# Low parts of the weights by a DMA that adds onto a tile written by ScalarE, instead of a subtraction on VectorE

## The chip, the cores and the metric

The kernel runs on one core of a Trainium2 chip. The core has TensorE (PE, matmuls, with PEld its weight loads), VectorE (DVE), ScalarE (ACT), GpSimd (POOL), SyncE (SP, here only issuing DMAs) and 16 DMA engines that all queues share. SBUF is the on-chip memory, PSUM holds matmul results, HBM is the chip's DRAM. The metric is the device time of one execution in microseconds; times are medians over runs. Each engine works through its own queue in order, and waits on semaphores of the others.

## The reference

Two transformer-like blocks run one after the other on 512 tokens of 1024 channels, all in float32. The first has two layers over the tokens and a context of 256 tokens (the context is updated only in layer 0), the second has one layer with a state-space (SSD) and a gated-delta branch.

```python
def trunk_layer(...):                      # first block, twice
    u  = (rmsnorm(x,  g_mix) * (1 + sc1)  + sh1)  @ w_in
    uc = (rmsnorm(cx, g_mix) * (1 + sc1c) + sh1c) @ w_in
    ...                                    # pooling, gated linear attention, attention
    x = x + ga1 * (mix @ w_out)
    x = x + ga2 * squared_relu_mlp(rmsnorm(x, g_mlp) * (1 + sc2) + sh2, w_up, w_down)
    if update_ctx:                         # the same for cx, 256 tokens
        ...
def squared_relu_mlp(h, w_up, w_down):
    return jnp.square(jax.nn.relu(h @ w_up)) @ w_down
def second_block(...):
    proj = h @ w_in[l]                     # 14400 columns
    ...                                    # SSD scan, gated delta rule, gates
    x = x + g1 * rmsnorm_2(merged @ w_out[l], norm_mix_post[l])
    y = jnp.square(jax.nn.relu(h @ w_mlp_up[l])) @ w_mlp_down[l]
    x = x + g2 * rmsnorm_2(y, norm_mlp_post[l])
```

Most of the arithmetic is products of activations with weight matrices of 1024 or 4096 rows.

## The kernel before

**Three products for one.** A float32 product is made of matmuls on the faster fp32r type. Each operand is split into a high part (rounded to fp32r) and a low part (the difference). `mm3` (lines 290 to 294) issues three matmuls: high times high (L292), a mixed product (L293), the other mixed product (L294).

**Weights.** A weight matrix is stored in DRAM as half tiles of 128 x 1024 floats (512 KB, 4 KB a partition), two of which make a group of 256 output columns. `whalf` (lines 273 to 283) brings one half: a DMA on SyncE's queue into `wraw` (three buffers), a rounding copy on ScalarE into `whi` (L281, two buffers), a subtraction raw minus high on VectorE into `wlo` (L282, two buffers). There are 503 halves in the run. Where the same weights serve two column parts, they are loaded once for each.

**Users.** `dense` takes weights as the stationary operand and activations of 512 or 256 columns as the moving one: per half 8 sets of three matmuls, and after the second half of a group two evacuations (for the up projections, ScalarE's relu, square and rounding copy, lines 1046, 1047 and 258). `tokens` takes the activations as stationary. The context MLP of layer 0, its output projection, and in the second block the output projection and the first groups of the up projection (`SPLITS`, `dense_parts`) run with 256 columns. Modulation vectors come from large weight rows too: by TensorE through `mraw` and `wraw` (L447, L444) or, in other stretches, by VectorE on rows that SyncE loads (L480, L484).

**Other traffic.** Block 2 writes many intermediates to DRAM and reads them back with another layout (on ScalarE's and SyncE's queues).

**GpSimd** does small work: it zeroes tiles (L723), takes the inverse roots of the norms (`root`, L392), and makes copies of one column that order buffers (L522).

**Order.** The code is written as a program; the Tile scheduler places the instructions on each engine's queue by a timeline it simulates. Weight splits are marked urgent (`urgent`), so they are placed early. The number of buffers of `wraw`, `whi` and `wlo` limits how far loads and splits run ahead of the matmuls.

## Time and profile before

| what | value |
|---|---|
| median of 3 runs | 3591.73 us (3591.07 to 3602.67) |
| profiled execution | 3592.06 us, its span 3590.1 us |
| granted TensorE clock, mean | 0.957 of 2.4 GHz |
| TensorE busy | 3392.4 us (94%) |
| VectorE busy | 2238.5 us (62%) |
| ScalarE busy | 1517.7 us (42%) |
| GpSimd busy | 58.5 us (2%) |
| DMA bytes | 492.55 MB, 137 GB/s over the span |

The profile is one execution. Busy times of an engine are sums over its instructions; matmuls overlap in the pipeline, so TensorE's busy time is not work at its peak. A wait is put down to the semaphore that came last. "Issue to landing" of a DMA is from its issue by the queue's engine to its completion.

### The profile page before, as it was taken

The numbers are of one execution on the slowest core, as the hardware profiler recorded it, in microseconds if no ns is written. First come the engines' busy times: TensorE is split into PE (matmuls) and PEld (weight loads), VectorE is DVE, ScalarE is ACT, GpSimd is POOL, SyncE is SP. The second block draws the span as 40 slices with busy tenths as digits, with TensorE's granted clock in tenths as the row PEclk, the third lists the DMA queues.
The fourth block names the chain that finished last, engine by engine and source line by source line (L and its number), as shares of the span: only waits on it lengthen the run. The fifth ranks groups of instructions, "written<-read, shape, count | busy, mean of one in ns | idle before, by whom it ended". The sixth has DMA issues, their size and how long they took to land.

```text
span 3590.1 us, 53732 instructions
## 1 busy us (share of the span) xinstructions
PE 3392.4 (94%) x20714; PEld 2823.2 (79%) x20714; DVE 2238.5 (62%) x4339; ACT 1517.7 (42%) x2675; POOL 58.5 (2%) x105
## 2 busy tenths in 40 slices
PE   7999999998999999989999999999899978999998
PEld 5787788887888797667888687788898757888886
DVE  3844787557533458866533779977866668663334
ACT  3523765453333355633333555453233323264333
POOL 0000000000000000000000000000000000000000
PEclk9799899999999998999999899999999979999999
DMA  6334123644622221036622356456456656453222
GB/s 226 119 125 151 54 80 104 222 135 147 194 100 96 99 71 34 7 117 195 201 95 91 120 180 179 147 165 196 144 180 193 213 185 188 154 185 130 94 94 76
DMA packets 268399, 492.55 MB, mean 137 GB/s; under 512 B 44912, under 2 KB 129904, under 8 KB 267888
## 3 DMA queue, kind: packets, MB, share of 16 engines
q1 hardware_dynamic: 214128, 447.17, 38.8%
q10 hardware_dynamic: 54016, 41.95, 3.5%
q8 instruction: 163, 2.67, 0.3%
q14 instruction: 92, 0.75, 0.1%
HBM read 431.22 MB, written 57.80 MB: 136 GB/s over the span
## 4 chain that ended last, share of the span: by engine, by line
PE 62%; issue 12%; DVE 11%; DMA 10%; ACT 3%; SPq 1%; POOL 0%; DVEq 0%; POOLq 0%; ACTq 0%
PE mm L292 15%; PE mm L293 15%; PE mm L294 15%; DMA mraw<-in_w_ada 2%; DVE wlo L282 2%; PE op L952 2%; PE sm L729 1%; DMA mraw<-in_w_late 1%; PE SC L447 1%; DVE AT L484 1%; DMA gG<-rowS 1%; PE SL L926 1%; ACT whi L281 1%; PE mm L590 1%; DVE svP L1498 1%
## 5 line engine op out<-in xcount | busy, mean ns | idle before, releaser
L282 DVE TENSOR_TENSOR wlo<-wraw,whi 128x1024 fp32r<-128x1024 f32 x503 | 614.2, 1221 | 519.2 <-ACT whi L281 514.9
L281 ACT ACTIVATE whi<-wraw 128x1024 fp32r<-128x1024 f32 x503 | 531.6, 1057 | 913.3 <-PE mm L293 727.4
L292 PE MATMUL mm<-h,whi 128*128 128x512 f32 (+1 forms) x2344 | 859.2, 369 | 23.7 <-ACT h L415 7.0
L293 PE MATMUL mm<-h,whi 128*128 128x512 f32 (+1 forms) x2344 | 852.2, 364 | 11.0 <-DVE h L416 9.8
L294 PE MATMUL mm<-h,wlo 128*128 128x512 f32 (+1 forms) x2344 | 835.7, 363 | 2.3 <-DVE wlo L282 2.0
L292 PEld LDWEIGHTS mm<-h,whi 128*128 128x128 f32 x2344 | 445.0, 190 | 108.7 <-ACT h L415 9.6
L293 PEld LDWEIGHTS mm<-h,whi 128*128 128x128 f32 x2344 | 446.1, 190 | 88.1 <-DVE h L416 17.9
L294 PEld LDWEIGHTS mm<-h,wlo 128*128 128x128 f32 x2344 | 444.0, 190 | 75.5 <-DVE wlo L282 4.8
L293 PE MATMUL mm<-wlo,h 128*128 128x256 f32 x1200 | 350.8, 293 | 16.7 <-DVE wlo L282 16.3
L292 PE MATMUL mm<-whi,h 128*128 128x256 f32 x1200 | 348.3, 293 | 10.9 <-ACT whi L281 7.8
L294 PE MATMUL mm<-whi,h 128*128 128x256 f32 x1200 | 343.9, 288 | 0.0
L293 PEld LDWEIGHTS mm<-wlo,h 128*128 128x128 f32 x1200 | 232.8, 194 | 28.7 <-DVE wlo L282 23.1
L292 PEld LDWEIGHTS mm<-whi,h 128*128 128x128 f32 x1200 | 231.6, 194 | 26.9 <-issue 11.0
L294 PEld LDWEIGHTS mm<-whi,h 128*128 128x128 f32 x1200 | 232.2, 194 | 14.1 <-issue 10.6
L292 PE MATMUL mm<-U,whi 128*128 128x512 f32 (+1 forms) x608 | 229.8, 379 | 1.3 <-DVE V L1076 1.3
L293 PE MATMUL mm<-U,whi 128*128 128x512 f32 (+1 forms) x608 | 227.0, 374 | 0.0
L294 PE MATMUL mm<-U,wlo 128*128 128x512 f32 (+1 forms) x608 | 222.9, 376 | 1.8 <-DVE wlo L282 1.8
L484 DVE SCALAR_TENSOR_TENSOR AT<-mraw,cst,AT 128x512 f32<-128x512 f32 x140 | 104.9, 750 | 96.7 <-DMA mraw<-in_w_ada 58.4
L292 PE MATMUL mm<-big,whi 128*128 128x512 f32 x384 | 154.2, 402 | 5.4 <-DVE fa L1826 2.4
L1286 DVE SCALAR_TENSOR_TENSOR fa<-fr,const,fa 128x511 f32<-128x511 f32 (+2 forms) x192 | 142.5, 750 | 26.0 <-ACT fa L1281 13.4
L293 PE MATMUL mm<-big,whi 128*128 128x512 f32 x384 | 153.4, 400 | 0.6 <-DVE big L259 0.6
L294 PE MATMUL mm<-big,wlo 128*128 128x512 f32 x384 | 150.0, 398 | 0.0
(570 smaller groups left out, 5059.4 us busy)
## 6 DMA issues: line engine op xcount, KB each, us to landing
wraw<-in_w_in SPq DMA_DIRECT2D x166, 512.0 KB, 3.5
wraw<-in_w_up SPq DMA_DIRECT2D x96, 512.0 KB, 3.3
wraw<-in_w_down SPq DMA_DIRECT2D x96, 512.0 KB, 3.4
mraw<-in_w_mod SPq DMA_DIRECT2D x96, 256.0 KB, 3.0
mraw<-in_w_ada SPq DMA_DIRECT2D x96, 256.0 KB, 2.9
wraw<-in_w_out SPq DMA_DIRECT2D x40, 512.0 KB, 3.3
wraw<-in_w_mlp_up SPq DMA_DIRECT2D x40, 512.0 KB, 3.3
mraw<-in_w_late SPq DMA_DIRECT2D x64, 256.0 KB, 2.8
```

What stands on the lines that cost most here:

```text
L281: nc.scalar.activation(hi, raw, AF.Copy)
L282: nc.vector.tensor_tensor(lo, raw, hi.bitcast(F32), op=ALU.subtract)
L292: nc.tensor.matmul(out, lh, rh, start=start, stop=False)
L293: nc.tensor.matmul(out, lh, rl, start=False, stop=False)
L294: nc.tensor.matmul(out, ll, rh, start=False, stop=stop)
L447: nc.tensor.matmul(ps[k % 4 * 32:k % 4 * 32 + 32, :256], st[:, k], raw[:, j * 256:(j + 1) * 256], start=(k < 4), stop=(k >= 4))
L484: nc.vector.scalar_tensor_tensor(acc, raw, st[:, k, 0:1], acc, op0=ALU.mult, op1=ALU.add)
L590: nc.tensor.matmul(ps[j * 32:j * 32 + 32], w[:, k * 32:k * 32 + 32], h[k][i % 2].bitcast(F32), start=(i == 0), stop=(i == 3))
L729: nc.tensor.matmul(gp[:, t], K[:, t], Q[:, t], start=True, stop=True)
L926: nc.tensor.matmul(at[i], qh[his], lo, start=False, stop=True)
L952: nc.tensor.matmul(op[j * 64:j * 64 + 64, pr * 128:(pr + 1) * 128], v[:, g * 64:(g + 1) * 64], pts[j][:, b * 128:(b + 1) * 128], start=(b ...
L1286: nc.vector.scalar_tensor_tensor(acc[:, d:], raw[:, :NL - d], w(j), acc[:, d:], op0=ALU.mult, op1=ALU.add)
```

## The change

The low part is no longer the difference of two tiles on VectorE. ScalarE reads the raw half a second time and writes its negated copy, rounded to fp32r in the same way, into `wlo`. Then a DMA on GpSimd's queue reads the same half from DRAM again and adds it onto `wlo`, which leaves raw minus high. `wraw` has two buffers instead of three, `wlo` three instead of two; the two other users of the `wraw` tag follow.

```diff
@@ whalf
-        raw = self.t([128, 1024], "wraw", 3)[:, :n]
+        raw = self.t([128, 1024], "wraw", 2)[:, :n]
         hi = self.t([128, 1024], "whi", 2, F32R)[:, :n]
-        lo = self.t([128, 1024], "wlo", 2, F32R)[:, :n]
+        lo = self.t([128, 1024], "wlo", 3, F32R)[:, :n]
         with self.urgent() if soon else nullcontext():
             nc.sync.dma_start(raw, self.A[name][i])
             nc.scalar.activation(hi, raw, AF.Copy)
-            nc.vector.tensor_tensor(lo, raw, hi.bitcast(F32), op=ALU.subtract)
+            nc.scalar.activation(lo, raw, AF.Copy, scale=-1.0)
+            nc.gpsimd.dma_start(lo, self.A[name][i], accum_op=ALU.add)
@@ modulation
-                raw = (self.spare.pop(0) if self.spare else self.t([128, 1024], "wraw", 3) if n == 4 else
+                raw = (self.spare.pop(0) if self.spare else self.t([128, 1024], "wraw", 2) if n == 4 else
@@ gla_proj
-        w = self.t([128, 1024], "wraw", 3)[:, :256]
+        w = self.t([128, 1024], "wraw", 2)[:, :256]
```

After line 282 the line numbers of the changed kernel are one higher: its L282 is ScalarE's second pass, L283 the adding DMA.

ScalarE's queue in the last groups of the context's up projection in layer 0 (256 columns), before; `ct` and `h` are the activations that are evacuated, the numbers count tiles:

```order
L281 ACTIVATE whi_6980<-wraw_6979 128x1024
L1046 ACTIVATE ct_6955<-mm_6905 128x256
L1047 ACTIVATE ct_6955<-ct_6955 128x256
L258 ACTIVATE h_932_5297<-ct_6955 128x256
L281 ACTIVATE whi_7010<-wraw_7009 128x1024
L1046 ACTIVATE ct_6972<-mm_6906 128x256
L1047 ACTIVATE ct_6972<-ct_6972 128x256
L258 ACTIVATE h_932_5297<-ct_6972 128x256
L281 ACTIVATE whi_7052<-wraw_7051 128x1024
```

The same place in the changed kernel:

```order
L282 ACTIVATE wlo_7086<-wraw_7084 128x1024
L1047 ACTIVATE ct_7029<-mm_6977 128x256
L1048 ACTIVATE ct_7029<-ct_7029 128x256
L281 ACTIVATE whi_7085<-wraw_7084 128x1024
L1047 ACTIVATE ct_7046<-mm_6978 128x256
L258 ACTIVATE h_932_5329<-ct_7029 128x256
L1048 ACTIVATE ct_7046<-ct_7046 128x256
L258 ACTIVATE h_932_5329<-ct_7046 128x256
L282 ACTIVATE wlo_7129<-wraw_7127 128x1024
L281 ACTIVATE whi_7128<-wraw_7127 128x1024
```

Of each half the negating pass now stands in front of the rounding pass, between evacuations of the groups before.

GpSimd's queue around the norm between the output projection and the MLP of the tokens in layer 0, before (`nr` is the inverse root of that norm):

```order
L674 MEMSET gst_8322 64x256 x2
L392 TENSOR_TENSOR nr_8061<-nv_8059,const_69 128x2
L873 COPY vc_8448<-U_294_1466 128x128 x2
L392 TENSOR_TENSOR nr_8787<-nv_8785,const_69 128x4
L423 MEMSET cst_14761 128x256
```

And the same norm in the changed kernel:

```order
L283 DMA wlo_8804<-in_w_out 128x1024
L283 DMA wlo_8835<-in_w_out 128x1024
L283 DMA wlo_8952<-in_w_up 128x1024
L283 DMA wlo_8983<-in_w_up 128x1024
L283 DMA wlo_9057<-in_w_up 128x1024
L393 TENSOR_TENSOR nr_8905<-nv_8903,const_69 128x4
L283 DMA wlo_9088<-in_w_up 128x1024
L283 DMA wlo_9162<-in_w_up 128x1024
```

The root now stands among the adding DMAs of the weights that are used before and after it.

## Rows read from the trace of the kernel before

**Rows 1.** The page's part 1: busy time, share of span, instructions.

```profile
span 3590.1 us, 53732 instructions
PE 3392.4 (94%) x20714; PEld 2823.2 (79%) x20714; DVE 2238.5 (62%) x4339; ACT 1517.7 (42%) x2675; POOL 58.5 (2%) x105
```

**Rows 2.** The page's part 4: chain that ended last, by engine, by line.

```profile
PE 62%; issue 12%; DVE 11%; DMA 10%; ACT 3%; SPq 1%; POOL 0%; DVEq 0%; POOLq 0%; ACTq 0%
PE mm L292 15%; PE mm L293 15%; PE mm L294 15%; DMA mraw<-in_w_ada 2%; DVE wlo L282 2%; PE op L952 2%; PE sm L729 1%; DMA mraw<-in_w_late 1%; PE SC L447 1%; DVE AT L484 1%; DMA gG<-rowS 1%; PE SL L926 1%; ACT whi L281 1%; PE mm L590 1%; DVE svP L1498 1%
```

**Rows 3.** Waits, whole span: who waited for whom, us, times, longest.

```profile
ACT whi L281 <- PE mm L293: 727.4, 285, 9.2
DVE wlo L282 <- ACT whi L281: 514.9, 248, 9.2
...
PE mm L293 <- DVE wlo L282: 16.3, 15, 2.3
...
PE mm L294 <- DVE wlo L282: 3.9, 3, 1.8
...
SPq L280 <- DVE wlo L282: 1471.7, 369, 26.8
```

**Rows 4.** Stretches: engines' busy us, clock, DMA share, GB/s; then L281 alone.

```profile
660.00:760.00 100.00, 98.79 (x816) 92.43 (x816) 56.27 (x80) 55.27 (x90) 0.00 (x0) 1.00 0.60 197
897.50:987.30 89.80, 87.87 (x402) 71.95 (x402) 53.79 (x76) 29.85 (x38) 0.32 (x1) 1.00 0.62 194
987.30:1077.00 89.70, 89.70 (x394) 73.59 (x393) 32.04 (x33) 32.29 (x42) 0.00 (x0) 1.00 0.29 99
...
660.00:760.00 100.00, 33.51 (x32) 1.00 0.60 197
897.50:987.30 89.80, 16.96 (x16) 1.00 0.62 194
987.30:1077.00 89.70, 16.98 (x16) 1.00 0.29 99
```

**Rows 5.** Groups of instructions by line and form: count, busy us, mean ns.

```profile
L282 DVE TENSOR_TENSOR wlo<-wraw,whi 128x1024 fp32r<-128x1024 f32 x503 | 614.2, 1221 | 519.2 <-ACT whi L281 514.9
L281 ACT ACTIVATE whi<-wraw 128x1024 fp32r<-128x1024 f32 x503 | 531.6, 1057 | 913.3 <-PE mm L293 727.4
...
L292 PE MATMUL mm<-h,whi 128*128 128x256 f32 x736 | 212.0, 292 | 2.5 <-ACT h L415 1.3 <-ACT whi L281 0.5 <-DVE h L1076 0.4
...
L292 PE MATMUL mm<-U,whi 128*128 128x256 f32 x96 | 26.8, 284 | 0.0
```

**Rows 6.** ScalarE in order of time, narrow up projection: start, duration, what.

```profile
684.16 0.39 ACT L1046 ACTIVATE ct<-mm 128x256 f32<-128x256 f32 x1 [0.47 <-PE mm L294]
684.58 0.42 ACT L1047 ACTIVATE ct<-ct 128x256 f32<-128x256 f32 x1
685.03 0.42 ACT L258 ACTIVATE U<-ct 128x256 fp32r<-128x256 f32 x1
```

**Rows 7.** DMA issues: count, KB each, median us from issue to landing.

```profile
wraw<-in_w_up SPq DMA_DIRECT2D x96, 512.0 KB, 3.3
...
wraw<-in_w_gdn_up SPq DMA_DIRECT2D x16, 512.0 KB, 4.8
```

**Rows 8.** One stretch of the start-up: engines' busy us, clock, DMA share, GB/s.

```profile
8.00:22.00 14.00, 12.58 (x84) 7.04 (x80) 3.28 (x10) 2.83 (x8) 0.71 (x1) 1.00 1.02 414
```

**Rows 9.** The page's part 2: DMA rate in 40 equal slices.

```profile
GB/s 226 119 125 151 54 80 104 222 135 147 194 100 96 99 71 34 7 117 195 201 95 91 120 180 179 147 165 196 144 180 193 213 185 188 154 185 130 94 94 76
```

**Rows 10.** GpSimd's longest wait by the waits view of that engine.

```profile
POOL nr L392 <- DVE nv L380: 1663.5, 12, 483.0
```

## The prediction

> **What bounds the kernel now.** I read the page's busy shares first. TensorE is busy 3392.4 of 3590.1 us [rows 1], so at most 198 us can be won by taking away what it waits for. The chain that ended last agrees: TensorE holds 62% of it, VectorE 11%, the DMAs 10% [rows 2]. Then the waits. Few of them end on TensorE: it waited 16.3 and 3.9 us for the low parts that VectorE makes. The weight stream in front of it is held back by its own buffers: ScalarE's rounding pass waits 727.4 us for matmuls to release a high-part buffer, VectorE 514.9 us for ScalarE, SyncE's load queue 1471.7 us for VectorE to release a raw buffer [rows 3]. So the subtraction, 503 pieces of 1221 ns, runs ahead of need; it costs VectorE 614.2 us, but TensorE only about 20.
>
> What decides is how far ahead a half tile is ready, against how long TensorE uses one. Two kinds of stretches matter. Where the matmuls have 512 columns, 16 halves pass in 89.7 us, 5.61 us each; where they have 256 columns (the context MLP, and the output projection and MLP of the second block in two column parts) 32 pass in 100 us, 3.1 us each [rows 4]. There are (736 + 96) / 8 = 104 such narrow halves, since a half takes eight matmuls of line 292 [rows 5].
>
> **The change part by part.** The sum is made against the profiled execution, 3592.06 us, which lies 0.3 us over the median of 3591.73, so the two are used as one.
>
> *VectorE loses 503 subtractions.* 614.2 us of its 2238.5 go [rows 1, 5]. On the path this gives the 20 us of waits for low parts [rows 3]. The chain holds 2% in that line and 9% in VectorE's other work [rows 2]; a shorter queue lets some of that come sooner. Bounds: 0 and the whole 2%, 72 us. I take 20 more, because the busiest VectorE stretches (inside the gated-delta and GLA steps) hold few halves. Together -40 (range -20 to -92).
>
> *ScalarE gains 503 passes.* Each is the same size and function as the rounding pass, 1057 ns [rows 5], 532 us in all. In wide stretches it is covered: ScalarE was busy 32.29 of 89.7 us there, and 16 x 1.06 = 17 are added [rows 4]. In the narrow up projections a half brings two passes and one column block's evacuation (0.39 + 0.42 + 0.42 us, [rows 6]): 2.11 + 1.23 = 3.35 us against 3.1. If nothing else were late this would cost 0.25 us in 48 halves (32 of the context MLP's up projection, 16 of block 2's), 12 us; it lies under the next term. The order shows the new pass standing in front of its own rounding pass, right behind the rounding pass of the half before.
>
> *The adding DMA.* 503 transfers of 512 KB come on GpSimd's queue, which held 2% of work [rows 1]. The trace of before has no DMA of that queue and none that adds. Its landing time L decides through this loop: the rounding pass of half i-2 starts when TensorE starts half i-3 (two high buffers), takes 1.06 us and, now that only two raw buffers exist, releases the one for half i; the load lands 3.3 us later [rows 7]; the negating pass takes 1.06; the DMA takes L; then half i can be used. From the start of half i-3 to that of half i are three halves, so 3P >= 1.06 + 3.3 + 1.06 + L = 5.4 + L. With the third raw buffer and the subtraction of before there was no such loop. In wide stretches 3P is 16.8: L up to 11.4 us is hidden. In narrow ones 3P is 9.3: L up to 3.9 us is hidden. The lower bound of L is a plain load of that size, 3.3 us: then it costs nothing. An upper bound is three of them, 9.9 us: P = 5.1, 2.0 x 104 = 208 us. I take two, 6.6 us, because the DMA has the row's bytes to fetch twice, once from HBM and once from the tile it adds onto: P = 4.0, 0.9 x 104 = **94 us**.
>
> The engines' throughput says the same. In the start-up burst the queues ran full, at 414 GB/s [rows 8]: 512 KB then take 1.27 us. A half with a load and two reads needs 3.81 us of all 16 engines. The narrow stretch moved 197 GB/s, 19.7 MB in 100 us; 32 halves are 16.8 MB of it [rows 4], the other 2.9 MB are 7 us, 0.22 a half: 4.03 us against 3.1. Whether the second read costs as much as the first, no row shows. The Trainium skill (Collectives: The Full Stack, the part "Why ReduceScatter is half of AllGather") says that an add in the DMA path costs no arithmetic time but two reads through one ring, 32.35 against 62.28 GB/s; by that page the estimate is 1.27 x 1.93 = 2.45 us a DMA, and the half would be at 3.9. No run here shows it yet.
>
> *The rest of the DMA traffic.* The DMAs on the chain are 10% of the span, 359 us [rows 2]: modulation rows, and the bounces through DRAM of block 2, in stretches that already move up to 213 GB/s [rows 9]. 512 KB land in 3.3 us where the traffic is light and took 4.8 in the up projections of block 2 where it is heavy [rows 7], 45% more. The added transfers load the engines further; bounds are 0 and 45% of 359 us, 162. I take 20%, **72 us**, since the bounces are small and only part of them meets an adding DMA.
>
> *Waits on GpSimd.* Each DMA waits there for the negating pass. Behind it in that queue stand later adding DMAs, the zeroing of score tiles and the 15 root steps of the norms; the reverse case, DMAs behind a root that waits (1663.5 us in 12 waits, [rows 10]), touches the halves after next, and TensorE needs them only after the norm. Order there is the scheduler's, and I cost it at 0; uncovered it is at most one L per root, 15 x 6.6 = 99 us.
>
> *Start-up.* Two raw buffers for three: five modulation tiles of 512 KB go through them before the first norm. One more load's landing, 4 us, shows (0 to 8).
>
> Sum: 3592 - 40 + 94 + 72 + 4 = 3722, called **3720 us**.
>
> **The rivals.**
> *Covered: faster.* If the adding DMA lands within 3.9 us, the narrow loop stays at 3.1 us, and the chain's DMAs lose little. For it: 414 GB/s are possible and the mean over the span is 137. Against it: a plain load through the idle SyncE queue already needs 3.3. It gives 3592 - 40 + 4 = 3556 us, with up to 36 us for ten per cent on the chain's DMAs 3592. The Trainium skill (DMA: Bandwidth & Descriptors, "Anatomy of one DMA — SWDGE (gpsimd) path") gives 2.0 us plus the bytes at 436 GB/s for a DMA issued by GpSimd; by that page a plain one of 512 KB would be an estimated 3.2 us, on this rival's side.
> *The DMA engines become the bound: much slower.* If an adding DMA occupies the engines as long as three reads or more, a half needs 1.27 + 3.81 = 5.08 us. Narrow: 5.3 with the other traffic, 2.2 x 104 = 229. Wide halves beside modulation loads (194 GB/s over 89.8 us are 17.4 MB, 9.0 more than their 16 halves, 1.37 us a half; [rows 4]) need 6.45 instead of 5.61: 0.84 us for some 120 halves in the ten wide slices of 180 GB/s and more after the start-up [rows 9], 101 us. The chain's DMAs pay 162. Sum 3592 - 40 + 229 + 101 + 162 + 4 = 4048 us. For it: the adding path is the one thing without a row. It decides from about 4 us of engine time per DMA.
> *No change.* The relief of 40 us is eaten by a landing time of some 4.6 us (P = 3.33, 0.2 x 104 = 24) and the chain's DMAs: 3590.
>
> **How the numbers follow.** Forecast case (slower, 3610 to 3850): 0.50. Engine-bound (3850 and up): 0.25. Covered: 0.17. No change: 0.08. A change of 0.3%, 11 us, is about what can be told from none here. So faster 0.17, same 0.08, slower 0.75. The range goes from 3555, which leaves out the half of the covered case where the relief is larger, to 4150, which leaves out the part of the engine-bound case with a costlier add: 0.08 and 0.10. The forecast case alone spans 3610 to 3850.
>
> **What would show it.** Right: in the narrow stretches the interval between rounding passes rises from 3.1 to about 4 us, TensorE's waits name the adding DMA, wide stretches without modulation keep 5.6 us a half, and VectorE's busy time falls by some 614 us with TensorE's busy time unchanged. The adding DMA's issue-to-landing time reads between 5 and 8 us. The engine-bound rival shows a DMA share near full and more than 5.6 us a half also in plain wide stretches; the covered one shows 3.1 us kept and no row of TensorE waiting for the DMA. Wrong also if the scheduler's new order moves waits into the attention or gated-delta stretches, which no term here holds.

## The result, and the profile after

The changed kernel takes 4038.51 us (median of 4 runs, 4010.13 to 4040.75); the kernel before took 3595.11 us beside it. The ratio is 1.121, with a 95% interval of 1.118 to 1.124: 443 us slower. The prediction was 3720 us, 128 us slower. The sign was right and the time lies inside the range, but the loss is three and a half times the forecast one. The total is near the 4048 us of the rival "the DMA engines become the bound"; whether it came about in that rival's way is shown below.

The page of the changed kernel, its parts 1, 3 and 4 (busy time; DMA queues with packets, MB and their share of 16 engines' span; the chain that ended last):

```profile
span 4035.9 us, 54644 instructions
PE 3536.1 (88%) x20714; PEld 2923.3 (72%) x20714; DVE 1678.5 (42%) x3836; ACT 1978.7 (49%) x3176; POOL 494.0 (12%) x608
...
q0 software_dynamic: 72432, 263.49, 38.3%
q1 hardware_dynamic: 214128, 447.17, 33.1%
...
PE 51%; DMA 25%; issue 12%; DVE 5%; ACT 3%; POOL 1%; SPq 0%; POOLq 0%; ACTq 0%; DVEq 0%
PE mm L295 13%; PE mm L293 13%; PE mm L294 13%; DMA wlo<-in_w_in 5%; DMA mraw<-in_w_ada 3%; DMA mraw<-in_w_late 2%; DMA wlo<-in_w_up 2%; PE sm L730 1%; DVE AT L485 1%; DMA gG<-rowS 1%; PE op L953 1%; DMA wraw<-in_w_in 1%; DMA wlo<-in_w_mlp_up 1%; DMA dv<-od 1%; DMA wlo<-in_w_out 1%
```

Against [rows 1], VectorE lost 560 us of busy time and ScalarE gained 461, somewhat less than the 614 and 532 that were costed. TensorE issues the same 20714 matmuls, yet its busy time grew by 144 us and its idle time by 302 (499.8 of the span for 197.7). The DMA share of the chain grew from 10% [rows 2] to 25%, and low parts now stand in it. q0 is the queue of the adding DMAs: 38.3% of 4035.9 us over 503 transfers is **3.07 us of all 16 engines for one**, against 1.57 us for 512 KB on q1, SyncE's queue, which is mostly loads (33.1%, 447.17 MB).

Who waited for whom in the changed kernel (us, times, longest); the first six are TensorE's longest:

```profile
PE mm L294 <- DMA wlo<-in_w_in: 96.6, 33, 8.8
PE mm L293 <- DVE V L1077: 31.8, 8, 6.4
PE mm L295 <- DMA wlo<-in_w_up: 30.4, 18, 3.6
PE mm L295 <- DMA wlo<-in_w_down: 27.4, 13, 6.9
PE mm L295 <- DMA wlo<-in_w_out: 21.8, 10, 4.5
PE mm L295 <- DMA wlo<-in_w_in: 21.1, 14, 4.0
...
DVE AT L485 <- DMA mraw<-in_w_ada: 119.6, 50, 6.1
...
DVE AT L485 <- DMA mraw<-in_w_late: 78.2, 33, 5.3
```

The longest wait is that of L294 for a low part, which is `tokens`' matmul; in [rows 3] the same wait (L293 there) was 16.3 us. The two waits of VectorE for modulation rows were 58.4 and 37.1 us before.

The same kernel's DMA issues (count, KB, median us from issue to landing) and its narrow matmuls by line and form:

```profile
wlo<-in_w_in POOLq DMA_DIRECT2D x166, 512.0 KB, 6.9
wraw<-in_w_up SPq DMA_DIRECT2D x96, 512.0 KB, 4.2
wlo<-in_w_up POOLq DMA_DIRECT2D x96, 512.0 KB, 6.1
...
mraw<-in_w_ada SPq DMA_DIRECT2D x96, 256.0 KB, 4.6
```

```profile
L293 PE MATMUL mm<-h,whi 128*128 128x256 f32 x736 | 229.6, 316 | 9.5 <-ACT h L258 2.7 <-ACT dq L249 1.5 <-ACT fa L1047 1.4
...
L295 PE MATMUL mm<-h,wlo 128*128 128x256 f32 x736 | 225.7, 315 | 67.7 <-DMA wlo<-in_w_out 21.8 <-DMA wlo<-in_w_mlp_up 18.5 <-DMA wlo<-in_w_down 14.9
```

An adding DMA lands 6.7 us after its issue (median of all, shown with the third experiment; by weight 6.1 to 8.1); 6.6 had been assumed. A modulation tile lands in 4.6 us where it took 2.9. The narrow matmul that took 292 ns [rows 5] takes 316: the same work, and the granted clock is lower (0.85 for 1.00 in the narrow core, below).

**Where the 443 us lie.** All kernels make the 503 halves in the same order, so the time between the starts of the same two rounding passes (L281) compares a stretch in two kernels. The table has the us of the kernel before and then the difference to it, for the changed kernel and three others that are told of in the experiments:

| halves | what runs there | before | after | only the DMA left out | DMA that doesn't add | token halves undone |
|---|---|---|---|---|---|---|
| 0 to 16 | start, first token groups | 79.5 | +37.0 | -4.8 | +12.4 | -0.3 |
| 16 to 40 | tokens, layer 0, then the context's output projection | 279.0 | +26.2 | -0.6 | +7.5 | +2.9 |
| 64 to 112 | context MLP, narrow | 204.9 | +85.7 | -6.7 | +39.5 | +68.5 |
| 120 to 152 | wide, modulation rows | 186.9 | +38.1 | -0.8 | +16.3 | +36.2 |
| 152 to 176 | plain wide | 132.3 | +3.2 | +1.5 | -0.1 | +1.0 |
| 176 to 208 | tokens, layer 1 | 418.6 | +34.8 | -3.9 | +3.4 | +20.2 |
| 208 to 240 | wide, modulation rows | 195.5 | +52.0 | -2.3 | +24.5 | +51.9 |
| 272 to 304 | block 2, first part | 217.3 | +24.0 | +3.1 | +12.4 | +30.4 |
| 304 to 416 | block 2, gated delta, state space | 918.1 | +69.9 | -38.7 | -9.6 | +38.1 |
| 416 to 456 | block 2, narrow | 162.0 | +62.8 | +11.7 | +27.3 | +54.6 |
| 456 to 502 | plain wide | 257.6 | +2.7 | 0.0 | +0.1 | +4.5 |

Five of these stretches, and the narrow core (halves 72 to 104), as the profile has them. A row has the stretch, its length, the busy us (and instructions) of TensorE, its weight loads, VectorE, ScalarE and GpSimd, then the granted clock, the DMA engines' share and GB/s. First before, in the order 16 to 40, 72 to 104, 120 to 152, 152 to 176, 208 to 240, 304 to 416:

```profile
119.55:398.54 278.99, 264.88 (x2038) 212.29 (x2036) 165.54 (x412) 112.07 (x245) 6.53 (x11) 0.91 0.38 124
649.15:755.04 105.89, 103.12 (x848) 95.59 (x847) 60.52 (x106) 53.83 (x86) 0.00 (x0) 1.00 0.61 204
871.51:1058.37 186.86, 184.05 (x824) 150.05 (x825) 98.09 (x129) 64.33 (x83) 0.32 (x1) 1.00 0.50 161
1058.37:1190.67 132.30, 132.30 (x579) 108.56 (x578) 46.48 (x48) 54.36 (x72) 0.00 (x0) 1.00 0.29 96
...
1609.27:1804.78 195.51, 189.69 (x856) 154.53 (x857) 118.78 (x164) 64.33 (x85) 0.00 (x0) 0.99 0.62 194
2221.23:3139.31 918.08, 856.98 (x5537) 735.47 (x5536) 689.71 (x1497) 333.67 (x555) 8.45 (x7) 0.96 0.56 175
```

The changed kernel, the same halves:

```profile
158.56:463.80 305.24, 280.38 (x2017) 220.73 (x2016) 134.77 (x360) 132.25 (x266) 26.73 (x35) 0.88 0.58 153
722.24:890.88 168.64, 133.70 (x903) 118.84 (x903) 20.66 (x53) 82.82 (x119) 26.82 (x31) 0.85 0.92 229
1024.12:1249.03 224.91, 197.71 (x825) 158.35 (x826) 61.87 (x98) 94.58 (x116) 28.05 (x33) 0.93 0.83 208
1249.03:1384.55 135.52, 132.81 (x579) 108.37 (x578) 17.09 (x24) 76.97 (x96) 20.76 (x24) 1.00 0.83 185
...
1837.99:2085.54 247.55, 206.13 (x857) 164.11 (x858) 83.04 (x132) 94.82 (x116) 27.78 (x32) 0.92 0.84 221
2530.20:3518.17 987.97, 874.34 (x5538) 744.45 (x5537) 566.31 (x1360) 435.70 (x669) 106.42 (x120) 0.96 0.85 223
```

Compare the second rows: in the narrow core 32 halves take 168.6 us instead of 105.9, 5.27 us each instead of 3.31, at a DMA share of 0.92 and a granted clock of 0.85, a mean over the two levels (1.2 and 2.4 GHz) where it was 1.00 before. The fourth rows: plain wide stretches keep 5.6 us a half even at a share of 0.83. The third and fifth rows: with modulation rows beside them the same wide halves take 7.0 and 7.7 us.

### The profile page after: what moved, and what is told of

Read it like the earlier page. It is cut to its first block, busy times and chain, and to the rows that moved or that the text cites. A ratio compares the mean times of both kernels' runs of the same rounds, so it can differ in the third digit from the quotient of the medians.

```text
span 4035.9 us, 54644 instructions
## 1 busy us (share of the span) xinstructions
PE 3536.1 (88%) x20714; PEld 2923.3 (72%) x20714; DVE 1678.5 (42%) x3836; ACT 1978.7 (49%) x3176; POOL 494.0 (12%) x608
## 3 DMA queue, kind: packets, MB, share of 16 engines
q0 software_dynamic: 72432, 263.49, 38.3%
q1 hardware_dynamic: 214128, 447.17, 33.1%
## 4 chain that ended last, share of the span: by engine, by line
PE 51%; DMA 25%; issue 12%; DVE 5%; ACT 3%; POOL 1%; SPq 0%; POOLq 0%; ACTq 0%; DVEq 0%
PE mm L295 13%; PE mm L293 13%; PE mm L294 13%; DMA wlo<-in_w_in 5%; DMA mraw<-in_w_ada 3%; DMA mraw<-in_w_late 2%; DMA wlo<-in_w_up 2%; PE sm L730 1%; DVE AT L485 1%; DMA gG<-rowS 1%; PE op L953 1%; DMA wraw<-in_w_in 1%; DMA wlo<-in_w_mlp_up 1%; DMA dv<-od 1%; DMA wlo<-in_w_out 1%
## 5 line engine op out<-in xcount | busy, mean ns | idle before, releaser
L295 PE MATMUL mm<-h,wlo 128*128 128x512 f32 (+1 forms) x2344 | 873.9, 377 | 109.8 <-DMA wlo<-in_w_up 30.4
L293 PE MATMUL mm<-h,whi 128*128 128x512 f32 (+1 forms) x2344 | 888.1, 382 | 53.1 <-DVE V L1077 14.5
L294 PE MATMUL mm<-h,whi 128*128 128x512 f32 (+1 forms) x2344 | 878.0, 375 | 10.3 <-DVE h L417 9.5
L281 ACT ACTIVATE whi<-wraw 128x1024 fp32r<-128x1024 f32 x503 | 530.2, 1054 | 664.8 <-PE mm L294 588.1
L282 ACT ACTIVATE wlo<-wraw 128x1024 fp32r<-128x1024 f32 x503 | 528.3, 1050 | 462.6 <-DMA wraw<-in_w_in 150.4
L295 PEld LDWEIGHTS mm<-h,wlo 128*128 128x128 f32 x2344 | 466.2, 200 | 199.2 <-DMA wlo<-in_w_up 36.6
L293 PEld LDWEIGHTS mm<-h,whi 128*128 128x128 f32 x2344 | 468.4, 201 | 144.4 <-issue 17.8
L294 PEld LDWEIGHTS mm<-h,whi 128*128 128x128 f32 x2344 | 469.7, 200 | 88.8 <-DVE h L417 16.7
L294 PE MATMUL mm<-wlo,h 128*128 128x256 f32 x1200 | 364.4, 304 | 96.8 <-DMA wlo<-in_w_in 96.6
L293 PE MATMUL mm<-whi,h 128*128 128x256 f32 x1200 | 366.9, 308 | 16.2 <-ACT whi L281 12.6
L295 PE MATMUL mm<-whi,h 128*128 128x256 f32 x1200 | 361.6, 302 | 0.0
L294 PEld LDWEIGHTS mm<-wlo,h 128*128 128x128 f32 x1200 | 248.6, 207 | 107.1 <-DMA wlo<-in_w_in 104.8
L283 POOL DMA_DIRECT2D wlo<-in_w_in x166 | 144.2, 869 | 1292.3 <-ACT wlo L282 1017.4
L293 PEld LDWEIGHTS mm<-whi,h 128*128 128x128 f32 x1200 | 248.0, 207 | 34.7 <-ACT whi L281 17.6
L295 PEld LDWEIGHTS mm<-whi,h 128*128 128x128 f32 x1200 | 248.0, 207 | 15.3 <-issue 11.6
L293 PE MATMUL mm<-U,whi 128*128 128x512 f32 (+1 forms) x608 | 234.6, 388 | 17.3 <-DVE V L1077 17.3
L294 PE MATMUL mm<-U,whi 128*128 128x512 f32 (+1 forms) x608 | 232.4, 385 | 0.0
L293 PE MATMUL mm<-big,whi 128*128 128x512 f32 x384 | 154.4, 403 | 1.6 <-ACT da L1796 0.9
```

What stands on the lines that cost most here:

```text
L281: nc.scalar.activation(hi, raw, AF.Copy)
L282: nc.scalar.activation(lo, raw, AF.Copy, scale=-1.0)
L283: nc.gpsimd.dma_start(lo, self.A[name][i], accum_op=ALU.add)
L293: nc.tensor.matmul(out, lh, rh, start=start, stop=False)
L294: nc.tensor.matmul(out, lh, rl, start=False, stop=False)
L295: nc.tensor.matmul(out, ll, rh, start=False, stop=stop)
```

## The experiments

**Which part of the change costs: buffers, ScalarE's pass, or the DMA?** Three kernels take it apart. (The diffs of this section show the lines that matter; the lines that shrink small work buffers to make room, and repeats of the same change, are left out.) The first gives the kernel before only the change's buffers.

```diff
-        raw = self.t([128, 1024], "wraw", 3)[:, :n]
+        raw = self.t([128, 1024], "wraw", 2)[:, :n]
-        lo = self.t([128, 1024], "wlo", 2, F32R)[:, :n]
+        lo = self.t([128, 1024], "wlo", 3, F32R)[:, :n]
```

> The kernel before with only the buffer counts of the change: two raw tiles, three low-part tiles, the subtraction still on VectorE. Theory A (the adding DMAs fill the 16 DMA engines) and theory B (too few raw buffers for the adding DMA's landing time) both expect 3595 us within 0.5%: without the DMA the loop needs only 5.4 + 1.2 us for three halves. If the counts alone cost something, it shows here: over 3615 us.

Measured: 3604.71 us against 3597.91, ratio 1.0018 (1.0003 to 1.0033). The buffers cost some 7 us.

The second is the changed kernel without its DMA:

```diff
             nc.scalar.activation(lo, raw, AF.Copy, scale=-1.0)
-            nc.gpsimd.dma_start(lo, self.A[name][i], accum_op=ALU.add)
```

> The changed kernel without the adding DMA: the low part is then the negated high part, so the product's correction is left out. VectorE's relief, ScalarE's second pass, the buffer counts and the new order are all in it. Both theories expect 3540 to 3580 us (relief of 40 us as predicted). If the second ScalarE pass or the new order costs time, it is over 3610 us, and that part of the 443 us lost has nothing to do with DMAs.

Measured: 3565.41 us, ratio 0.9906 (0.9882 to 0.9930). Buffers, ScalarE's second pass and VectorE's relief together are a gain of 34 us, which lies between halves 304 and 416 (table). ScalarE's pass is not quite free in it: TensorE's wait for the rounding pass grew (11.7 us with the buffers alone; here the kernel before, then this one), and the narrow halves 416 to 456 took 11.7 us longer (4.1 with the buffers alone).

```profile
PE mm L292 <- ACT whi L281: 9.0, 8, 4.5
```

```profile
PE mm L292 <- ACT whi L281: 37.6, 44, 2.7
```

What the DMA adds to this is 4038.5 - 3565.4 = 473 us.

In the third the DMA is issued in the same place and moves the same bytes, but writes instead of adding:

```diff
-            nc.gpsimd.dma_start(lo, self.A[name][i], accum_op=ALU.add)
+            nc.gpsimd.dma_start(lo, self.A[name][i].bitcast(F32R))
```

> The changed kernel with a plain load in place of the adding DMA, same queue, same bytes from DRAM: the low part is then the raw tile, so the sum is left out. One read instead of two. Theory A: the queue's share of the engines falls from 38% to about 20%, and half of the excess goes, 3780 to 3850 us; the stretch from the 65th to the 113th half (204.8 us before, 290.7 after) takes 240 to 255. Theory B: the landing falls from 6.7 to about 4.5 us, three narrow halves need some 10 us of ready time, and nearly all of the excess in that stretch goes: under 225 us.

Measured: 3732.48 us, ratio 1.0372 (1.0343 to 1.0402). Its page, part 3 and DMA issues, and the times from issue to landing of all 503:

```profile
q0 software_dynamic: 72432, 263.49, 23.5%
...
wlo<-in_w_up POOLq DMA_DIRECT2D x96, 512.0 KB, 4.6
...
DMA to landing us min/median/max: 3.4/4.6/8.6
```

The same line of the changed kernel:

```profile
DMA to landing us min/median/max: 4.8/6.7/10.8
```

23.5% of its span of 3725.2 us over 503 is 1.74 us of engine time, and it lands in 4.6 us. Issuing one occupies GpSimd for 527 ns; one that adds, for 865. So of the 473 us a plain second read costs 167 and the adding another 306, and each of the lossy stretches of the table shares in both. The stretch of halves 64 to 112 took 244 us, in the upper of the two ranges expected: even a plain read is not covered there. The total fell below the 3780 to 3850 us of theory A. Engine time and landing time fell together here, so this run doesn't tell the two apart; the next ones do. (It also reads its source as the tile's type; whether that counts was not tried alone.)

**The narrow halves: a loop through buffers, or full engines?** The forecast had both as one number. A third raw buffer breaks the loop of the forecast (paid for with one buffer less of `P`, `cs` and `jy`):

```diff
-        raw = self.t([128, 1024], "wraw", 2)[:, :n]
+        raw = self.t([128, 1024], "wraw", 3)[:, :n]
```

> The changed kernel with three raw tiles; for the space, the attention's weights P have one buffer instead of two, one scratch tile of the context norm one and one tile of the gated-delta join one, so only the stretch from the 65th to the 113th half is read, which holds none of these but the norm. Theory B: a third raw tile breaks the loop (four halves for 5.4 us and the landing), and the stretch falls from 290.7 to under 235 us. Theory A: the same bytes and reads pass through the same engines, and it stays within 15 us of 290.7.

Measured: 3993.13 us, ratio 1.1097 (1.1059 to 1.1135). Halves 64 to 112 take 267.5 us, between the two expectations: the loop was a part of it. The next kernel has a third high buffer too (and pays with `vc`, `cr`, `E`, `fu`, `fy`), so only single stretches of it are read:

```diff
-        raw = self.t([128, 1024], "wraw", 2)[:, :n]
-        hi = self.t([128, 1024], "whi", 2, F32R)[:, :n]
+        raw = self.t([128, 1024], "wraw", 3)[:, :n]
+        hi = self.t([128, 1024], "whi", 3, F32R)[:, :n]
```

> The changed kernel with three raw, three high and three low buffers (2, 2, 3 in the change), paid for by one buffer less of seven small work tags, so only its stretch of narrow halves and its token stretches are read. In the narrow stretch (halves 72 to 104) a half took 3.31 us before, 5.27 in the changed kernel, 4.77 with a third raw buffer alone. Theory 'engines': a half needs 1.57 us of all 16 engines for its load, 3.07 for the adding DMA and 0.22 for other traffic, 4.86; the third raw buffer has already reached that, and a third high buffer changes nothing: 4.6 to 5.0. Theory 'loop': the load no longer waits for matmuls at all, what is left is the low buffer (2P at least 1.06 + 6.7 us): 3.9 to 4.3. Token stretches: if late high parts kept TensorE there, halves 16 to 40 and 176 to 200 come down by 10 us or more from 305 and 383; otherwise they stay.

Measured: 4091.74 us in all, ratio 1.1375 (1.1324 to 1.1427). The narrow core, halves 72 to 104, first with the third raw buffer alone, then with the third high buffer as well:

```profile
703.47:856.18 152.71, 127.60 (x913) 107.50 (x912) 20.60 (x53) 84.41 (x118) 26.82 (x31) 0.94 1.01 268
```

```profile
736.29:890.18 153.89, 125.23 (x886) 107.69 (x886) 22.98 (x76) 82.85 (x117) 27.62 (x32) 0.94 1.00 262
```

4.77 and 4.81 us a half, at a DMA share of 1.01 and 1.00: the engines are full, and more buffers bring nothing. The demand worked out for this, 1.57 + 3.07 + 0.22 = 4.86 us, is what is measured. Of the 1.96 us that a narrow half lost, 1.5 are full engines and 0.5 the loop. The token stretches didn't gain from the third high buffer: 16 to 40 took 324.9 us, 176 to 208 took 460.6. (The 176 to 200 of the expectation can't be compared: with three high buffers the rounding of half 200 starts ahead of some 170 us of other work that it used to follow.) Whether late high parts hold them up is not shown by this, since this kernel has one `E` buffer instead of two, and `E` is used in those very stretches.

**The modulation stretches: full engines, or two small buffers?** Four `mraw` buffers instead of two, paid for with `P` and `cs`:

```diff
-                       self.t([128, 512], "mraw", 2))
+                       self.t([128, 512], "mraw", 4))
```

> The changed kernel with four buffers of 128x512 for the modulation rows (mraw) instead of two, paid for by one buffer less of two small work tags. In the stretches in which VectorE or TensorE consumes these rows beside wide halves, 32 halves took 186.9 us before and 224.9 after (halves 120 to 152), 195.5 and 247.5 (halves 208 to 240). Theory 'landing time': two buffers in a loop with loads that now land in 4.4 to 4.6 us instead of 2.8 to 2.9; two more buffers hide that: 120 to 152 falls to 187 to 200, 208 to 240 to 195 to 210, total about -75 us, 3960. Theory 'traffic': the stretch needs all 16 DMA engines (32 loads of 1.57 us, 32 adding DMAs of 3.07 us are 148 us of full engines, and the modulation rows come on top), so buffers change nothing: 120 to 152 stays above 215 and 208 to 240 above 238, DMA share 0.9 or more.

Measured: 3957.04 us, ratio 1.1000 (1.0975 to 1.1024), 81 us less than the changed kernel. Halves 120 to 152 and 208 to 240 in it:

```profile
1000.77:1196.86 196.09, 187.09 (x816) 152.11 (x815) 58.49 (x91) 93.93 (x115) 27.98 (x33) 0.97 0.91 234
...
1792.27:1993.96 201.69, 189.77 (x850) 153.22 (x849) 81.12 (x127) 93.27 (x114) 27.67 (x32) 0.99 0.96 263
```

Its waits of VectorE for these rows:

```profile
DVE AT L485 <- DMA mraw<-in_w_ada: 50.1, 25, 6.0
...
DVE AT L485 <- DMA mraw<-in_w_late: 31.5, 14, 3.7
```

75 of the 90 us of these two stretches are gone although each tile lands later still (5.3 us) and the engines move more (263 GB/s for 221). It was landing time: with two buffers VectorE gets two tiles per round trip, and the round trip had grown from 2.9 to 4.6 us. A clock of 0.92 went back to 0.99 with it.

**The token stretches.** The forecast had no term for them. First a fourth low buffer (paid for with `P`, `cs`, `jy`):

```diff
-        lo = self.t([128, 1024], "wlo", 3, F32R)[:, :n]
+        lo = self.t([128, 1024], "wlo", 4, F32R)[:, :n]
```

> The changed kernel with four low-part buffers instead of three (paid for by one buffer less of three small work tags). In the token stretches (context as stationary operand, two halves used together) the time between the starts of the same rounding passes rose from 279.0 to 305 us (halves 16 to 40), from 355.1 to 382.5 (halves 176 to 200) and from 330.6 to 403.2 (halves 344 to 384). Theory 'latency': tokens keeps both halves of a group until the group ends, so with three low buffers the adding DMA of the second half of the next group starts only when the group before has ended, and its 6.7 us lie open. Then the fourth buffer brings 344 to 384 down to 330 to 360 and the two others to within 10 us of before; in all about -90 us, 3950. Theory 'traffic': the DMA engines move what they can in these stretches, so the fourth buffer changes nothing: 344 to 384 stays at 395 or more, total within 15 us of 4038. The high part and raw buffers stay at two, so if the loop through those is what is late, the result is that of the second theory with a DMA share well under 0.9.

Measured: 4155.38 us, ratio 1.1551 (1.1521 to 1.158), slower than the changed kernel, which neither theory expected. The wait aimed at did go, from 96.6 us to:

```profile
L294 PE MATMUL mm<-wlo,h 128*128 128x256 f32 x1200 | 350.2, 292 | 32.6 <-DMA wlo<-in_w_in 32.5
```

But ScalarE's queue in a plain wide stretch of this kernel (start, duration, what, idle before) shows a new order:

```profile
3955.57 1.06 ACT L282 ACTIVATE wlo<-wraw 128x1024 fp32r<-128x1024 f32 x1 [2.05 <-DMA wraw<-in_w_mlp_up]
...
3957.71 1.05 ACT L282 ACTIVATE wlo<-wraw 128x1024 fp32r<-128x1024 f32 x1
...
3960.47 1.04 ACT L281 ACTIVATE whi<-wraw 128x1024 fp32r<-128x1024 f32 x1
3963.12 1.06 ACT L281 ACTIVATE whi<-wraw 128x1024 fp32r<-128x1024 f32 x1 [1.61 <-PE mm L294]
```

With low buffers to spare the scheduler puts two negating passes ahead of two rounding passes; in the changed kernel the two kinds alternate there. Both raw buffers are then held until a high buffer comes free, loads come in pairs, and even plain wide halves go from 5.6 to 6.2 us. So this run shows that the low parts can be had in time for tokens, and not what that is worth. The next one says more: for the 86 halves that `tokens` uses the change is undone.

```diff
+            if sub:
+                nc.vector.tensor_tensor(lo, raw, hi.bitcast(F32), op=ALU.subtract)
+            else:
                 nc.scalar.activation(lo, raw, AF.Copy, scale=-1.0)
                 nc.gpsimd.dma_start(lo, self.A[name][i], accum_op=ALU.add)
@@ tokens
-        w = self.wload(name, g)
+        w = self.wload(name, g, sub=True)
```

> The changed kernel with the change undone for one kind of user: halves that tokens uses (activations as the stationary operand, both halves of a group in use until its end) get their low part by the subtraction on VectorE, as before; all others keep the negating pass and the adding DMA, with the buffers of the change. Theory 'tokens had no cover': the low part is late there by its own 6.7 us of landing, and TensorE's clock falls with each wait. Then TensorE waits 10 to 25 us for low parts in that form of matmul (96.6 in the changed kernel, 16.3 before), the stretches of halves 16 to 40 and 176 to 208 come back to within 10 us of before (279.0 and 418.6; 305.2 and 453.4 in the changed kernel), 304 to 416 (918.1, 988.0) falls by 25 us or more, the others stay; total 3930 to 3970. Rival 'traffic': the stretches are longer because adding DMAs of neighbouring halves and the bounces share the engines; then the three stretches keep over half of what they lost, and the total is 4000 or more.

Measured: 3916.24 us, ratio 1.0893 (1.085 to 1.0935): 122 us less than the changed kernel, more than expected, from a sixth of the halves. The form of `tokens` in it (L297 is the matmul that was L294):

```profile
L296 PE MATMUL mm<-whi,h 128*128 128x256 f32 x1200 | 350.0, 295 | 10.8 <-ACT whi L281 9.8 <-DVE fa L1667 0.8
L297 PE MATMUL mm<-wlo,h 128*128 128x256 f32 x1200 | 349.6, 292 | 22.7 <-DVE wlo L283 22.5
L298 PE MATMUL mm<-whi,h 128*128 128x256 f32 x1200 | 346.1, 289 | 0.0
```

The wait for low parts is back at 22.5 us, 74 less than in the changed kernel, and the three token forms are busy 1045.7 us instead of 1092.9 (292 ns a matmul instead of 305). These two make 121 of the 122 us. The run takes 86 adding DMAs off the engines along with the wait, so it doesn't quite rule out their traffic; but the DMA share of halves 16 to 40 had been 0.58. By the last column of the table the start (0 to 16) and tokens of layer 0 are back at before, 304 to 416 gained 32 us; layer 1's stretch kept 20 of its 35, so there more than the token halves is late. A landing time of 4.6 instead of 6.7 us has most of the same effect (table, the DMA that doesn't add: +7.5 and +3.4, with 18.6 us of that wait). An estimate from these landing times is that a low part of `tokens` has a cover between the two.

**Is the relief of VectorE to be had without the DMA?** GpSimd subtracts all halves, in the kernel before:

```diff
-            nc.vector.tensor_tensor(lo, raw, hi.bitcast(F32), op=ALU.subtract)
+            nc.gpsimd.tensor_tensor(lo, raw, hi.bitcast(F32), op=ALU.subtract)
```

> The kernel before with one word changed: the subtraction that makes the low part runs on GpSimd instead of VectorE, with no added DMA, no added ScalarE pass and the buffers of before (3, 2, 2). It gives VectorE the same relief as the change. Theory: what the change lost is all DMA, what it gained is VectorE's relief, worth 34 us as the run without the adding DMA showed. If one subtraction on GpSimd takes less than 3.1 us (the pace of the narrow halves) and does not slow VectorE, the time is 3555 to 3575 us, with halves 384 to 416 some 45 to 60 us shorter than before. Rival: GpSimd is slower than that; a subtraction of x us with two low buffers makes the 104 narrow halves x us each, at 4 us 94 us more, 3660, and token and start-up stretches later too. Second rival: GpSimd and VectorE slow one another when both read SBUF; then VectorE's other work gets longer per instruction (its mean durations show it) and 384 to 416 gains little.

Measured: 3784.82 us, ratio 1.0524 (1.0496 to 1.0553). Two groups of the page's part 5:

```profile
L282 POOL TENSOR_TENSOR wlo<-wraw,whi 128x1024 fp32r<-128x1024 f32 x503 | 1237.6, 2464 | 2136.1 <-ACT whi L281 2008.7
...
L484 DVE SCALAR_TENSOR_TENSOR AT<-mraw,cst,AT 128x512 f32<-128x512 f32 x140 | 156.5, 1118 | 109.8 <-DMA mraw<-in_w_ada 65.5
```

2.46 us is under the 3.1 us of the narrow pace, and the narrow stretch 64 to 112 lost only 10 us. But VectorE's L484, 750 ns in the kernel before, takes 1118: the second rival's sign. Its other sign failed: halves 384 to 416 did gain, 53.4 us, as the theory has it. They were outweighed by the 101.6 us that 304 to 384 lost and some 20 each in several other stretches. TensorE's own waits for low parts from GpSimd came to 36 us; how the rest divides was not tried. Next, GpSimd for the 32 halves of block 2's up projections alone:

```diff
+            (nc.gpsimd if name in ("w_gdn_up2", "w_ssm_up2") else nc.vector).tensor_tensor(lo, raw, hi.bitcast(F32), op=ALU.subtract)
```

> The kernel before, with only the 32 halves of block 2's two up projections (gated delta and state space, halves 384 to 416) subtracted on GpSimd; the other 471 stay on VectorE. Theory: the relief of the change sits in this stretch alone (286.1 us before, 44.5 to 63.3 us less in every kernel that takes the subtraction from VectorE). There a half has 8.9 us before, so that even a subtraction of 4 us on GpSimd is in time: 3535 to 3560 us, faster than before by 1 to 1.6%. Rival: the relief comes from the whole of VectorE's queue running ahead in the earlier steps, not from this stretch: then within 10 us of before. Second rival: GpSimd's copies that order buffers, and its zeroing of tiles, stand behind subtractions that wait, and the time rises.

Measured: 3618.14 us, ratio 1.0053 (1.0036 to 1.0069). Halves 384 to 416 took 312.2 us, 26 more than before. VectorE's operations of this stretch:

```profile
L1827 DVE TENSOR_TENSOR V<-V,fa 128x512 f32<-128x512 f32 x22 | 19.3, 875 | 0.4
...
L1826 DVE TENSOR_TENSOR fa<-mm,fa 128x512 f32<-128x512 f32 x23 | 15.8, 687 | 36.0 <-PE mm L294 36.0
```

L1827 has both inputs in SBUF and took 686 ns before; L1826 has one of them in PSUM and stayed at 687. The Trainium skill (SBUF — State Buffer, "SBUF: two separate sides") says that VectorE, on an operation with two SBUF inputs, and a GpSimd operation that reads SBUF exclude one another for a whole instruction; these two rows agree with it. The relief was eaten by that: 32 subtractions of 1.22 us had left VectorE in this stretch, and it was busy 204.2 us in it after 205.6 before. Why the stretch got 26 us longer stays open, and so did whether the relief is local. The change for these 32 halves only says more (with the change's buffers):

```diff
+            if name in ("w_gdn_up2", "w_ssm_up2"):
+                nc.scalar.activation(lo, raw, AF.Copy, scale=-1.0)
+                nc.gpsimd.dma_start(lo, self.A[name][i], accum_op=ALU.add)
+            else:
+                nc.vector.tensor_tensor(lo, raw, hi.bitcast(F32), op=ALU.subtract)
```

> The change made for the 32 halves of block 2's two up projections alone (halves 384 to 416), with the change's buffers (2, 2, 3); the other 471 halves keep the subtraction on VectorE. Theory 'relief is local': the stretch, 286.1 us before, falls by 25 to 45 us, since in the changed kernel it fell by 44.5 in spite of a DMA share of 0.94; with 7 us for the buffers the total is 3560 to 3580. Rival 'relief is the queue running ahead': in the changed kernel half of VectorE's 64 steps of the state-space rows (line 1732 there) were done before this stretch began, because VectorE had no subtractions to make earlier; then removing the 32 here gives at most their own 39 us of busy time where VectorE is late, the 98 us of engine time of 32 adding DMAs slow the bounces through DRAM in the same stretch, and the total is 3600 to 3640.

Measured: 3620.48 us, ratio 1.0071 (1.0046 to 1.0096). Halves 384 to 416 took 17 us longer than before, 344 to 384 took 12 longer. The local theory falls: the same 32 adding DMAs stand in this stretch of the changed kernel, where it fell by 44.5 us. That VectorE's queue as a whole runs ahead can be seen in its 128 instructions of the state-space rows (L1731 of the kernel before). Ahead of half 384, 64 of them had started in the kernel before and also in the two kernels that relieve this stretch alone, 100 in the changed kernel (36 of the 64 that were left, the half that the expectation speaks of) and 98 without its DMA. So the 34 us come from work done earlier, and were not to be had in one stretch.

**A version that beats both.** The modulation loop was close to its limit before the change as well. The kernel before with four `mraw` buffers:

```diff
-                       self.t([128, 512], "mraw", 2))
+                       self.t([128, 512], "mraw", 4))
```

> The kernel before with four buffers of 128x512 for modulation rows instead of two, paid for by one buffer less of two small work tags; the low part stays on VectorE. In the changed kernel these two buffers brought halves 208 to 240 from 247.5 to 201.7 us. Theory: before, the same loop was only just hidden: halves 120 to 152 and 208 to 240 take 5.84 and 6.11 us a half against 5.5 in stretches without modulation rows, so up to 10 and 19 us can be won, in all 3565 to 3585 us. Rival: what is late there before is not the rows' landing (2.8 us) but VectorE's own work on them; then those stretches stay within 4 us, and the smaller work buffers cost up to 10 us: 3590 to 3605.

Measured: 3584.38 us against 3598.58, ratio 0.9963 (0.9947 to 0.9979): 0.4% faster than before, 11% than the changed kernel. Its stretches 120 to 152 and 208 to 240 gained 5.4 and 7.9 us, about half of the 10 and 19 that were expected at most; 16 to 40 and 40 to 64 gained 11 and 12, 64 to 112 and 176 to 208 lost 9 and 12, perhaps to the smaller work tags.

## Why the prediction was wrong, point by point

**What failed first is a stretch that the loop was never written for.** "In wide stretches 3P is 16.8: L up to 11.4 us is hidden" holds for plain wide halves, which kept 5.6 us. The step went on as if all halves that aren't narrow were of that kind. `tokens` keeps both halves of a group until its end, and 86 halves are of that form; undoing the change for them alone took back 122 us, for which the sum held nothing. [rows 3] had the hint: the longest of TensorE's waits for low parts, 16.3 us, is on L293; `mm3` has the weights' low part in L293 only where `tokens` calls it, and in L294 only where `dense` does. A subtraction of 1.2 us was already late there, and a DMA of 6.7 could only be later. The 37 us of the start are of this kind too (they went with the token halves). The 4 us costed there for a load that comes late through two raw buffers didn't show: with the change's buffers alone the start took 2.8 us less.

**The rest of the DMA traffic: the term was too small by more than half.** Forecast 72 us, bounds 0 to 162. The two modulation stretches lost 90. In block 2 (304 to 416), the kernel without the DMA gained 38.7 and the changed one lost 69.9, so the DMA costs 109 there; 32 of these went with the token halves, and 77 are the bounces through DRAM and the rest, which no run separates. 90 + 77 = 167. The step that failed is "I take 20%" of the DMAs on the chain: it scaled a landing time. Where a loop of two buffers feeds VectorE, a landing time of 2.9 that becomes 4.6 us lengthens the whole stretch, not only the pieces that stood on the chain. Four buffers took 75 of the 90 back.

**The narrow halves: mechanism right, price too low.** Forecast 94 us; measured 86 + 63 = 149, of which 25 went with the token halves (last column; six of those lie in 64 to 112), so 124. That is fewer halves at a higher price: of the 104, the 24 halves 40 to 64 pass beside other work at 8.4 us each and lost nothing (202.0 us before, 202.2 after), while one in the narrow core lost 1.96 us and not 0.9. L was taken as 6.6 us and is 6.7. The size of two reads for an add was nearly right: 3.07 us is 1.96 times the 1.57 of q1 in the same run, and 1.76 times the 1.74 of the plain DMA on its own queue. The Trainium skill (Collectives: The Full Stack, "Why ReduceScatter is half of AllGather") gives 1.93 for its two reads; the first of these ratios agrees with it, the second lies below. What was mis-sized is the read itself: 1.27 us, from a burst at 414 GB/s [rows 8]. With 1.57, a half needs 4.86 us of full engines instead of 4.03, and 4.77 were measured as soon as the loop was out of the way. Part 3 of the page of before would have said so:

```profile
q1 hardware_dynamic: 214128, 447.17, 38.8%
```

38.8% of 3590.1 us for 447.17 MB is 1.63 us per 512 KB. The other 0.5 us a half are the loop, which keeps the engines from filling (share 0.92 for 1.01): its load landed in 4.2 to 5.6 us (medians by weight of those with narrow halves), not in 3.3.

**TensorE's busy time was taken as fixed.** "TensorE's busy time unchanged" is wrong by 144 us with the same matmuls. Where TensorE began to wait the granted clock fell in most stretches, to 0.85 in the narrow core and 0.92 in halves 208 to 240 against 1.00 and 0.99 before, and both go up again where a kernel takes waits away (0.94, 0.99); halves 304 to 416 kept 0.96. So a third of the 446 us between the two spans is slower matmuls. No term of the sum held that. It is not all a loss of its own: in the narrow core, where TensorE was busy 31 us longer (with 55 matmuls more), the pace is that of the DMA engines, and faster matmuls would have waited for them.

**What was right.** VectorE's relief: -40 forecast, -34 measured with buffers and ScalarE's pass. The size is luck: it is not at the rows named (the waits for low parts), and it lies between halves 304 and 416, around the gated-delta steps of which the forecast expected little. ScalarE's pass is covered in wide stretches, and costs some us in narrow ones, as was said. The order on GpSimd's queue cost nothing that shows: TensorE waited 8.2 us for the roots of the norms, and 6.4 before. Plain wide stretches stayed at 5.6 us, so the engine-bound rival, which wanted three reads' worth of engine time and full engines everywhere, did not come about. In narrow stretches alone it came nearer than the forecast: the engines are the bound there, and its 5.3 us a half stand against 5.27, though with 3.07 us and not 3.81 for the add. That its total of 4048 is near is chance: its terms were 229, 101 and 162 where 124, 90 and 77 were measured, and tokens fill the gap. The covered rival wanted the adding DMA to land within 3.9 us; even a plain one on the same queue took 4.6.

Measured terms: -34 + 124 + 90 + 77 + 122 = 379 of the 443 us. Another 24 are in halves 272 to 304, for which no experiment was made, 20 stay in the tokens of layer 1 when their own low parts are in time, and some 20 are spread over the other stretches. All three stay open.

## What to carry to other kernels

Before a step's landing time is called hidden, list every kind of consumer with the number of buffers it holds and for how long; here the one whose wait showed up even in the profile of before, though short, was the one without cover. Price a transfer by its queue's share of the engines over the whole span (time by bytes), not by the best burst, and look at what TensorE's clock loses where it begins to wait. And a loop of two small buffers that feeds another engine pays the longer landing time on each round: two more of them were worth more (81 us) than a third large one (45 us).

## What the runs showed of the hardware

An adding DMA of 512 KB from DRAM onto SBUF took 3.07 us of 16 engines and landed in 6.7 us (median; 4.8 to 10.8); without the add 1.74 and 4.6 us (3.4 to 8.6), on the same queue. Its issue held GpSimd for 865 ns, without the add for 527. A subtraction of 128x1024 on GpSimd took 2.46 us, twice VectorE's 1.22, and beside such subtractions VectorE's operations with two SBUF inputs took up to half as long again (750 to 1118 ns, 686 to 875), one with an input in PSUM the same 687 ns.
